# First span's mixers fed through DRAM; the gate projections of both of its blocks as seven-product quads

## The chip, the cores and the metric

The kernel runs on one core of one Trainium2 chip. The metric is the device time of one execution in microseconds (us), lower is better. A core has TensorE (PE; its weight loads are shown apart as PEld), VectorE (DVE), ScalarE (ACT), GpSimd (POOL) and SyncE (SP), which here issues every DMA. SBUF holds the working tiles, PSUM eight banks of 128 x 512 float32, DRAM the inputs, the output and what is put away.

## The reference, cut to what matters

One layer of a streaming encoder, 2048 tokens, width 1024, float32:

```python
xn = rms_norm(x)
aq, ak, av, mq, mk, mv, mo, i, f, ga, gm = split(xn @ w_in)  # 512 x 7, 4, 4, 1024, 1024
A = chunk_band_attention(aq, ak, av, rel_bias)     # 8 heads of 64, own chunk of 64 + 8 before
M = mlstm(silu(conv(mq)), silu(conv(mk)), mv, i, f)          # 4 heads of 128, recurrent
M = sigmoid(mo) * headwise_rms_norm(M)
y = sigmoid(ga) * (A @ w_att_proj) + sigmoid(gm) * (M @ w_mlstm_proj)
x = x + y @ w_out
x = x + relu(rms_norm(x) @ w_up) ** 2 @ w_down
out = rms_norm(x)
```

A and M are 512 wide; ga, gm and y 1024.

## The kernel before

**Blocks and spans.** The 2048 tokens are four blocks of 512 (b = 0 to 3), held feature-major: 128 features on the partitions, 512 tokens along the row. Blocks 0 and 1 are the first span (s = 0), blocks 2 and 3 the second.

**Exactness.** Each float32 operand is split in a high part (rounded to the float32r format) and the rest. A product is three matmuls: high x high, high x low, low x high (`mm3`). A weight tile of 128 x 1024 is loaded into `wraw` (four buffers) and split into `wsp` (three buffers) by one ScalarE and one VectorE pass (lines 427 and 429), in the order that `weights()` lists.

**Two ways to multiply.** A *plain* tile (`feature_tile`, `token_tiles`, `pair_tile`) multiplies one block by one weight tile: 24 matmuls of 128x512 (lines 488 to 490). A *quad* (`quad`, line 571) treats two blocks, two halves of the contraction and two halves of the outputs as a 2 x 2 block product and forms it with seven products for eight. Each of the seven is a weight tile (a sum or difference of four loaded ones, `quad_w`) by an operand (a sum or difference of the four input quarters, A[m][k]); the outputs are sums that `combine` gathers from the banks. One quad gives two output tiles in each half for both blocks, in 7 x 24 = 168 matmuls where plain tiles take 8 x 24 = 192. Its 28 operand tiles lie in `rpool`, which has 28 slots in all.

**Stages.** `dense()` drives TensorE:

1. for b = 0, 1: plain tiles for v, mv, then q, k, mq, mk, mo interleaved (`evac_q`, `evac_k`, `evac_conv`, `evac_og`), then eight plain tiles for ga (`evac_ga`), then the eight projection tiles of A and M (`pair_tile`, with `evac_att` and `evac_rec`), whose results are stored in the DRAM tensor `proj`. Attention (`attention`, `head`, `unit`) and recurrence (`recurrence`, `rec_head`) of the block run beside these tiles, from q, k, v and conv outputs that stay in SBUF slots; block 1 also needs k and v of block 0, which are put away in DRAM (`kspill`, `vspill`);
2. two quads for gm over both blocks (`take_xn`, `after_gate`). Their combining loads the two stored projections, merges them with gm and gives y;
3. two quads for w_out (`take_y`, `after_out`), which add x and store x2;
4. eleven quads or token quads for the whole of w_in on blocks 2 and 3 (`IN_ORDER`, `after_in`, `after_vm`); every result is stored in DRAM (`qfar`, `kfar`, `mvfar`, `mfar`, `gate`);
5. the first span's w_up quads and its w_down products (`down`). Beside `down` run attention and recurrence of blocks 2 and 3, fed from DRAM: `attention_far`, `head_far`, `recurrence_far`, `load_rec`; their results go to DRAM too (`mix`);
6. `project(2)` and `project(3)`: the mixers' results are loaded and split (`take_mix`), projected, merged with the stored gates (`load_gates`, `merge`); under `project(3)` the w_out operands of the second span are formed (`take_y_low`, `take_y_rest`);
7. the second span's w_out, w_up, w_down and final norm (`final`).

**Order.** Every piece of work is a generator that yields what it needs: an engine with an estimated time, a wait for events, or slots of a pool. The class `Flow` runs them at build time as a list scheduler with a clock for each engine and writes the instructions in the order that it finds, so the order on each engine is fixed in the program. Priorities: `dense` has 5 and is passed by work with lower numbers; other threads' matmuls are delayed by a slack of 800 ns after they become ready, so that dense matmuls stand between. Pools: `rpool` 28 slots of two 128x512 parts, `ctx` 16 and `temp` 6 of 128x516 float32, `sc` 4, eight PSUM banks.

Of the kernel before, what the change touches and what calls it, by code (L numbers as in the profile page):

```python
# [44 lines left out]
N_W = 44  # L45
# [4 lines left out]
Q_VM, Q_IN = N_Q, dict(q=N_Q + 2, mq=N_Q + 3, ga0=N_Q + 4, k=N_Q + 5, mk=N_Q + 6, ga1=N_Q + 7, mo=N_Q + 8)  # L50
IN_ORDER = ("gm0", "gm1", "q", "mq", "vm0", "ga0", "k", "vm1", "mk", "ga1", "mo")
# [163 lines left out]
def dve_ns(n):  # L215
    return 70 + 1.042 * n
# [7 lines left out]
class Layer:  # L224
# [99 lines left out]
    def weights(self):  # L324


        part = lambda q, m: ("part", (q, m))
        for b in range(2):
            yield from (("plain", n) for n in range(N_W))
        for q in range(N_G):  # L330
            yield "quad", (q, False)
        yield from (part(q, m) for q in range(N_G, N_G + N_O) for m in range(7))
        for name in IN_ORDER:
            if name[:2] == "vm":
                yield from (part(Q_VM + kk, m) for m in range(7) for kk in range(2))
            else:
                yield "quad", (int(name[2]) if name[:2] == "gm" else Q_IN[name], False)
        for s in range(NS):
# [10 lines left out]
            if s == 0:  # L349
                for _ in range(2):  # L350
                    yield from (("plain", N_W - 8 + 4 * x + j) for j in (0, 2, 1, 3) for x in range(2))
# [277 lines left out]
    def dense(self):  # L629
        fl = self.fl  # L630
        none = [None] * KT
        for b in range(2):
# [3 lines left out]
            fl.spawn(self.attention(b), 1)  # L636
            fl.spawn(self.recurrence(b), 1)
# [12 lines left out]
            yield from self.token_tiles(vs, none, lambda t, bk: self.evac_mv(b, t, bk))  # L650
            self.banks.want = 2
            if b == 0:
                fl.put(self.rpool, *vs)
# [4 lines left out]
            if b == 0:  # L658
                fl.spawn(self.norm_in(1), 3)
# [7 lines left out]
            if b == 1:  # L667
                G = self.operands()
                for k in range(4):
                    fl.spawn(self.take_xn(k, *G), 2)  # L670
            for q in range(N_G, N_G + N_O if b == 0 else 0):
                fl.spawn(self.sum_w(q), 3)
            self.banks.want = 3
            for x, evac in ((0, self.evac_att), (1, self.evac_rec)):
                for j in range(4):
                    yield "wait", B["mix_ev"][4 * x:4 * x + 4]
                    bks = yield from self.pair_tile(B["mix"][4 * x:4 * x + 4], none)
                    for n in range(2):
                        fl.spawn(evac(b, 2 * j + n, bks[n]), 1)
                fl.put(self.rpool, *B["mix"][4 * x:4 * x + 4])  # L680

        self.banks.want = 0
        O, X, U = self.operands(), self.operands(), self.operands()
        for i in range(N_G):
            if i == N_G - 1:
                for k in range(2):
                    fl.spawn(self.take_y(0, k, *O), 2)
            yield from self.quad(*G, self.after_gate(i, O), release=i == N_G - 1)
        for i in range(N_O):
# [5 lines left out]
            yield from self.quad(*O, self.after_out(0, i, None), release=i == N_O - 1)  # L695

        for i, name in enumerate(IN_ORDER):
# [10 lines left out]
            else:  # L708
                yield from self.quad(*X, self.after_in(name), release=last)
        for s in range(NS):  # L710
# [25 lines left out]
            for p, m in enumerate(ORDER):  # L736
                if p == 1:
                    fl.spawn(self.residual(s), 2)
                if s == 0 and p == len(ORDER) - 1:
                    O = self.operands()  # L740
# [4 lines left out]
            if s == 0:  # L745
                yield from self.project(2)
                for k in range(4):
                    fl.spawn(self.take_y_low(k, *O), 2)
                U = self.operands()
                go = Event()  # L750
                first_out = self.after_out(1, 0, U, go)
# [1776 lines left out]
```

## Time and profile before

| what | value |
|---|---|
| time, median of 3 | 2848.65 us |
| lowest and highest | 2846.07 and 2852.96 us |
| the profiled execution's own time | 2843.84 us |
| its span (first to last instruction) | 2842.1 us |
| mean granted TensorE clock | 0.998 |
| busy: PE, PEld | 2804.1, 2342.9 us |
| busy: DVE, ACT, POOL | 2028.9, 1549.7, 48.6 us |
| DMA traffic | 612.03 MB, 215 GB/s |

The profile comes from one execution. Busy time is the time in which an engine has at least one instruction in work; matmuls overlap, so the mean duration of one is longer than their distance. A row of a group names the source line, the engine, the operation, output<-inputs by tile name, the shape and the count, then busy us, mean ns of one, idle us of the engine just before them, and what ended that idle time. In the view of stages every stretch (start:end in us) has the busy time of each engine. Line numbers are those of the kernel before.

### The profile page before, as it was taken

What the parts mean: (1) busy time and instruction counts of PE and PEld (TensorE: products, weight loads), DVE (VectorE), ACT (ScalarE), POOL (GpSimd) and SP (SyncE); (2) the same over time, 40 slices, a digit from 0 to 9 for tenths busy, and PEclk for the clock granted to TensorE, in tenths of its full rate; (3) what the DMA queues carried; (4) which work ended last, traced back from release to release, by engine and by line L of the source; (5) the groups of instructions that cost most, each with busy time, mean ns of one, the idle gap of its engine ahead of it and who ended that gap; (6) DMA issues with size and microseconds to landing.
All of it is one profiled execution on the core that took longest, in us unless ns stands there. A gap on an engine that the chain in (4) does not pass through costs nothing.

```text
span 2842.1 us, 39060 instructions
## 1 busy us (share of the span) xinstructions
PE 2804.1 (99%) x13576; PEld 2342.9 (82%) x13576; DVE 2028.9 (71%) x3767; ACT 1549.7 (55%) x2677; POOL 48.6 (2%) x108
## 2 busy tenths in 40 slices
PE   8999999999999999999999999999999999999998
PEld 7888888888878887888887888888887888888887
DVE  6886478877896766886667788889578644455565
ACT  4664366755444535575556566665435655555444
POOL 0000000000000000000000000000000000000000
PEclk9999999999999999999999999999999999999999
DMA  6337733367756677588778977866597655566563
GB/s 213 100 96 247 254 99 103 104 212 238 263 196 210 205 258 242 195 296 310 265 270 270 283 237 225 249 217 219 204 306 230 213 200 194 198 238 212 188 223 134
DMA packets 280869, 612.03 MB, mean 215 GB/s; under 512 B 31456, under 2 KB 47968, under 8 KB 280672
## 3 DMA queue, kind: packets, MB, share of 16 engines
q1 hardware_dynamic: 280672, 609.55, 65.0%
q8 instruction: 106, 1.74, 0.3%
q14 instruction: 91, 0.75, 0.1%
HBM read 431.17 MB, written 178.26 MB: 214 GB/s over the span
## 4 chain that ended last, share of the span: by engine, by line
PE 80%; DVE 9%; DMA 5%; ACT 3%; issue 2%; POOL 0%; SPq 0%; POOLq 0%; DVEq 0%; ACTq 0%
PE bank L571 36%; PE bank L488 12%; PE bank L489 12%; PE bank L490 12%; PE bank L1243 2%; DVE wsp L429 2%; PE bank L1314 2%; PE bank L1283 1%; DMA wsum<-ctx 1%; DVE sc L1289 1%; ACT wsp L427 1%; DMA ctx<-in_wf 1%; DMA r<-u 1%; PE bank L599 1%; DVE r L1319 1%
## 5 line engine op out<-in xcount | busy, mean ns | idle before, releaser
L571 PE MATMUL bank<-r,wsp 128*128 128x512 f32 x5208 | 1188.6, 390 | 4.6 <-DVE ctx L1837 2.2
L571 PEld LDWEIGHTS bank<-r,wsp 128*128 128x128 f32 x5208 | 975.7, 188 | 210.6 <-DVE ctx L1837 3.8
L429 DVE TENSOR_TENSOR wsp<-wraw,wsp 128x1024 fp32r<-128x1024 f32 x461 | 563.2, 1222 | 352.5 <-ACT wsp L427 336.0
L427 ACT CAST wsp<-wraw 128x1024 fp32r<-128x1024 f32 x461 | 483.8, 1050 | 468.6 <-PE bank L571 196.7
L488 PE MATMUL bank<-r,wsp 128*128 128x512 f32 x1600 | 639.8, 400 | 2.3 <-ACT tmp L2379 2.3
L490 PE MATMUL bank<-r,wsp 128*128 128x512 f32 x1600 | 625.0, 391 | 0.0
L489 PE MATMUL bank<-r,wsp 128*128 128x512 f32 x1600 | 624.6, 390 | 0.0
L490 PEld LDWEIGHTS bank<-r,wsp 128*128 128x128 f32 x1600 | 300.3, 188 | 64.8
L488 PEld LDWEIGHTS bank<-r,wsp 128*128 128x128 f32 x1600 | 301.0, 188 | 54.4 <-ACT tmp L2379 3.0
L489 PEld LDWEIGHTS bank<-r,wsp 128*128 128x128 f32 x1600 | 301.4, 188 | 51.4
L986 ACT CAST r<-r 128x512 fp32r<-128x512 f32 x240 | 146.4, 621 | 86.2 <-DMA r<-u 71.5
L991 DVE TENSOR_TENSOR r<-r 128x512 fp32r<-128x512 f32 x240 | 160.3, 687 | 38.4 <-ACT r L986 37.3
L1837 DVE TENSOR_TENSOR ctx<-bank,ctx 128x512 f32<-128x512 f32 x174 | 119.0, 687 | 81.1 <-PE bank L571 79.3
L1298 ACT ACTIVATE sc<-sc,scs 128x640 f32<-128x640 f32 (+4 forms) x128 | 97.5, 762 | 85.1 <-DVE scs L1295 82.6
L1829 ACT COPY ctx<-bank 128x512 f32<-128x512 f32 x174 | 101.1, 582 | 61.5 <-PE bank L571 54.8
L2198 ACT ACTIVATE ctx<-ctx 128x512 f32<-128x512 f32 x96 | 60.6, 631 | 103.0 <-DVE ctx L1837 103.0
L396 DVE TENSOR_TENSOR ctx<-ctx,ctx 128x512 f32<-128x512 f32 x112 | 76.3, 688 | 55.4 <-DMA ctx<-in_wf 39.8
L1289 DVE CUSTOM_DVE_ANT_0 sc<-bank,bias 128x320 f32<-128x320 f32 (+3 forms) x240 | 105.4, 460 | 12.2 <-PE bank L1283 9.7
L1243 PE MATMUL bank<-r,r 128*128 128x256 f32 (+1 forms) x672 | 109.2, 283 | 4.6 <-DVE r L1319 3.5
L1243 PEld LDWEIGHTS bank<-r,r 128*128 128x128 f32 x672 | 99.2, 191 | 16.6 <-DVE r L1319 7.0
L1319 DVE TENSOR_TENSOR r<-bank,r 128x512 fp32r<-128x512 f32 (+1 forms) x168 | 96.3, 594 | 17.0 <-ACT r L1317 16.1
L1317 ACT CAST r<-bank 128x512 fp32r<-128x512 f32 (+1 forms) x168 | 81.7, 518 | 25.1 <-PE bank L1314 23.1
(291 smaller groups left out, 2850.2 us busy)
## 6 DMA issues: line engine op xcount, KB each, us to landing
wraw<-in_wf SPq DMA_DIRECT2D x170, 512.0 KB, 4.2
wraw<-wsum SPq DMA_DIRECT2D x136, 512.0 KB, 4.0
r<-u SPq DMA_DIRECT2D x224, 256.0 KB, 4.1
wraw<-in_w SPq DMA_DIRECT2D x104, 512.0 KB, 3.9
u<-ctx SPq DMA_DIRECT2D x128, 256.0 KB, 2.6
ctx<-in_wf SPq DMA_DIRECT2D x112, 256.0 KB, 3.9
wsum<-ctx SPq DMA_DIRECT2D x112, 256.0 KB, 4.3
u<-tmp SPq DMA_DIRECT2D x96, 256.0 KB, 3.0
```

The costliest lines, as they stand in the source:

```text
L427: nc.scalar.copy(w[:, 0], raw)
L429: nc.vector.tensor_sub(w[:, 1], raw, w[:, 0].bitcast(F32))
L488: mm(ps, lh, rh, start=first, stop=False)
L489: mm(ps, lh, rl, start=False, stop=False)
L490: mm(ps, ll, rh, start=False, stop=last)
L571: mm(ps, wv[:, x, k, n], a[:, y], start=new and k == 0 and x == y == 0, stop=k == 3 and x == 1, skip_group_check=True)
L986: self.nc.scalar.copy(dst[:, 0], src)
L991: self.nc.vector.tensor_sub(dst[:, 1], src, dst[:, 0].bitcast(F32))
L1243: nc.tensor.matmul(bk[:, c0:c0 + w], st, sl[:, x, o:o + w], start=n == 0, stop=n == total - 1)
L1289: nc.vector.tensor_tensor_reduce(out=e[:, x * w:x * w + w], in0=bks[x][:, :w], in1=br[:, j0 + x * w:j0 + x * w + w], op0=ALU.add, op1=ALU. ...
L1319: nc.vector.tensor_sub(slot[:, 1, :o], bk[:, :o], slot[:, 0, :o].bitcast(F32))
L1837: nc.vector.tensor_add(t[:, o:o + 512], ps, t[:, o:o + 512])
```

## The change

- **Blocks 0 and 1 use the far mixers.** `attention`, `head`, `evac_q`, `evac_k`, `spill_k`, `recurrence` go; `attention_far`, `head_far`, `recurrence_far`, `load_rec` serve all four blocks. After their plain tiles, v, q, k, mv, the conv outputs and mo are stored in DRAM (`evac_v`, `evac_parts`, `evac_mv`, `evac_conv` with `conv_far`, `evac_og`) and loaded per head. The tiles' order changes: q and k first, then the conv inputs, then mo; block 1's mv tiles come after its q and k. The conv's history and the recurrence's gates are chained over all blocks in the same way.
- **ga as quads.** The 16 plain ga tiles go. Four quads, ga0, ga1, gm0, gm1, run over both blocks (`GATES`), from the operands that gm alone used; they are loaded in two parts (`take_low` for the first two products, `take_rest`).
- **Block 0's projection** runs after both blocks' dense tiles and is stored raw (`keep_proj`). The combining of gm loads it with the stored ga and merges the three (`merge_kept`).
- **Block 1's projection** runs after the four quads by `project(1)`, as in the second span, and `project_span` holds what both spans now share.
- **norm_in(1)**, the first norm of block 1, is spawned before block 0's q and k tiles, in `ctx` instead of `sc`, and takes its `rpool` slots one by one (`x_room`) instead of waiting for block 0's.

The core of the diff:

```diff
         for b in range(2):
...
-            fl.spawn(self.attention(b), 1)
-            fl.spawn(self.recurrence(b), 1)
+            fl.spawn(self.attention_far(b), 1)
+            fl.spawn(self.recurrence_far(b), 1)
...
             for j in range(4):
-                for fn in (self.evac_q, self.evac_k, self.evac_conv_q, self.evac_conv_k, self.evac_og):
+                for name in ("q", "k"):
                     (bk,) = yield from self.feature_tile(xs, none if b > 0 or j > 0 else B["xs_done"])
-                    fl.spawn(fn(b, j, bk), 1)
...
+                    fl.spawn(self.evac_parts(b, j, name, bk), 1)
+            if b > 0:
+                yield from self.token_tiles(vs, none, lambda t, bk: self.evac_mv(b, t, bk))
+            for j in range(4):
+                for g in (j, MH + j):
+                    (bk,) = yield from self.feature_tile(xs, none)
+                    fl.spawn(self.evac_conv(b, g, bk), 1)
...
-            for j in range(8):
+            for j in range(4):
                 (bk,) = yield from self.feature_tile(xs, none)
-                fl.spawn(self.evac_ga(b, j, bk), 1)
+                fl.spawn(self.evac_og(b, j, bk), 1)
...
+        fl.spawn(self.take_mix(0), 1)
+        for j in (0, 2, 1, 3):
+            for x in range(2):
+                some = slice(4 * x, 4 * x + 4)
+                bks = yield from self.pair_tile(self.blk[0]["mix"][some], self.blk[0]["mix_ev"][some])
+                for n in range(2):
+                    fl.spawn(self.keep_proj(x, 2 * j + n, bks[n]), 1)
...
-        for i in range(N_G):
-            if i == N_G - 1:
-                for k in range(2):
-                    fl.spawn(self.take_y(0, k, *O), 2)
-            yield from self.quad(*G, self.after_gate(i, O), release=i == N_G - 1)
+        for name in GATES:
+            last = name == GATES[-1]
+            if last:
+                fl.spawn(self.take_mix(1), 1)
+            yield from self.quad(*G, self.after_in(name, 0), release=last)
+        O, first_out = yield from self.project_span(0, None)
...
+    def merge_kept(self, j, t):
...
+        yield "wait", [self.proj_ev[0][j], self.proj_ev[1][j], self.g_ev[0, 0, j]]
+        got = yield "get", self.temp, 3
+        m, a, g = (x[:, :512] for x in got)
+        for to, src in ((m, self.projd.ap()[1, j]), (a, self.projd.ap()[0, j]), (g, self.gd[0].ap()[0, j])):
+            yield "sp", 900, 3000
+            nc.sync.dma_start(to, src)
+        yield "dve", dve_ns(512)
+        nc.vector.scalar_tensor_tensor(t5, t5, 1.0, m, op0=ALU.add, op1=ALU.mult)
+        yield "dve", dve_ns(512)
+        nc.vector.scalar_tensor_tensor(a, g, 1.0, a, op0=ALU.add, op1=ALU.mult)
+        yield "dve", dve_ns(512)
+        nc.vector.tensor_add(t5, t5, a)
...
+    def project_span(self, s, U):
...
+        O = self.operands()
+        if s > 0:
+            yield from self.project(2 * s)
+        for k in range(4):
+            fl.spawn(self.take_low(k, *O, self.ypd[2 * s], self.yp_ev[2 * s], 0.5), 2)
+        go = Event()
+        after = self.after_out(s, 0, U, go)
+        for k in range(4):
+            fl.spawn(self.take_rest(k, *O, self.ypd[2 * s:2 * s + 1], self.yp_ev[2 * s:2 * s + 2], 0.5, self.y3[s]), 1)
+        yield from self.project(2 * s + 1, go)
+        return O, after
```

`head_far` now loads the k of every block by its two halves:

```diff
-        for n, x in ((0, b - 1), (1, b)):
-            if x < 2:
-                yield "wait", [self.blk[x]["k_spilt"][h]]
-                yield "sp", 900, 2000
-                nc.sync.dma_start(kf[:, n], self.kdram[x].ap().bitcast(F32)[h])
-            else:
-                yield "wait", [self.k_ev[x, j]]
-                yield "sp", 900, 2000
-                for a in range(2):
-                    nc.sync.dma_start(kf[a * 64:a * 64 + 64, n], self.kfar[x].ap()[j, a, rows])
+        for n, x in ((0, b - 1), (1, b)) if b > 0 else ((1, b),):
+            yield "wait", [self.k_ev[x, j]]
+            yield "sp", 900, 2000
+            for a in range(2):
+                nc.sync.dma_start(kf[a * 64:a * 64 + 64, n], self.kfar[x].ap()[j, a, rows])
```

More of the change, by code (lines that the diff above doesn't have):

```diff
@@ L44 @@
 NS = NB // 2
-N_W = 44
+N_W = 36
 N_G, N_O, N_F = 2, 2, 8
@@ L50 @@
 Q_VM, Q_IN = N_Q, dict(q=N_Q + 2, mq=N_Q + 3, ga0=N_Q + 4, k=N_Q + 5, mk=N_Q + 6, ga1=N_Q + 7, mo=N_Q + 8)
+GATES = ("ga0", "ga1", "gm0", "gm1")
 IN_ORDER = ("gm0", "gm1", "q", "mq", "vm0", "ga0", "k", "vm1", "mk", "ga1", "mo")
@@ L349, in weights @@
             if s == 0:
-                for _ in range(2):
-                    yield from (("plain", N_W - 8 + 4 * x + j) for j in (0, 2, 1, 3) for x in range(2))
+                yield from proj + proj
     def loader(self):
@@ L708, in dense @@
             else:
-                yield from self.quad(*X, self.after_in(name), release=last)
+                yield from self.quad(*X, self.after_in(name, 1), release=last)
         for s in range(NS):
@@ L1578, in rec_head @@
+        yield from self.store(self.mfar[b].ap()[2 * MH + h], d5, self.m_ev[b, 2 * MH + h], self.ctx, dst)
     def rec_head(self, b, h):
@@ L2463, in _layout @@
         tiles += [feat(w_in, _X[n] + j * P) for n in ("q", "k", "mq", "mk", "mo")]
-    tiles += [feat(w_in, _X["ga"] + j * P) for j in range(8)]
     for w in (w_att, w_ml):
```

534 lines of the change are left out of this document (162 added, 372 removed).

## The prediction

> **What bounds the kernel now.** I read the page first: the totals by engine and the chain that ended last.
>
> ```profile
> span 2842.1 us, 39060 instructions
> PE 2804.1 (99%) x13576; PEld 2342.9 (82%) x13576; DVE 2028.9 (71%) x3767; ACT 1549.7 (55%) x2677; POOL 48.6 (2%) x108
> ...
> PEclk9999999999999999999999999999999999999999
> ...
> PE 80%; DVE 9%; DMA 5%; ACT 3%; issue 2%; POOL 0%; SPq 0%; POOLq 0%; DVEq 0%; ACTq 0%
> ```
>
> TensorE works from end to end at the full granted clock, and stands idle for 2842.1 - 2804.1 = 38.0 us in all. The other engines count only where they make it wait. So two things are to be found: how many matmuls go, at what pace, and where the new order makes TensorE wait. For both I cut the span by stage; the borders come from the timeline of TensorE. Columns: stretch, its length, then busy us and instructions of PE, PEld, DVE, ACT, POOL, then granted clock, share of the DMA engines and GB/s.
>
> ```profile
> 80.00:215.00 135.00, 133.53 (x759) 114.36 (x758) 113.62 (x333) 92.33 (x224) 8.18 (x20) 1.00 0.30 95
> ...
> 380.00:556.00 176.00, 174.96 (x1024) 152.62 (x1023) 152.08 (x426) 123.04 (x277) 11.61 (x19) 1.00 0.32 104
> ...
> 645.00:721.00 76.00, 76.00 (x337) 62.94 (x336) 64.27 (x88) 42.45 (x66) 0.00 (x0) 1.00 0.78 254
> 721.00:797.00 76.00, 76.00 (x344) 62.96 (x343) 68.51 (x98) 33.27 (x47) 0.00 (x0) 1.00 0.70 238
> ...
> 1520.00:1950.00 430.00, 422.25 (x2419) 365.03 (x2418) 350.43 (x945) 270.21 (x593) 12.55 (x36) 1.00 0.79 243
> 1950.00:2128.00 178.00, 174.59 (x839) 146.00 (x838) 121.50 (x173) 77.31 (x111) 3.25 (x2) 1.00 0.74 249
> 2128.00:2216.00 88.00, 85.60 (x375) 69.70 (x374) 76.70 (x113) 51.40 (x77) 0.00 (x0) 1.00 0.71 231
> ```
>
> In order: attention of block 0 (its first to its last score), attention of block 1, the two gm quads of the first span, its two w_out quads, attention and recurrence of blocks 2 and 3 (fed through DRAM), their projections with the end of the down products, and the w_out quads of the second span. The second span already runs the form that the change gives to the first, so it is the nearest row for nearly every new cost.
>
> **The matmuls.** A plain tile is 24 matmuls of 128x512 (8 k by 3 products), a quad 7 products x 2 x 4 x 3 = 168. Out go 8 ga tiles in each of two blocks, 16 x 24 = 384; in come two quads (ga0, ga1), 336. That is 48 fewer, and the order of instructions of the two kernels shows the same: 10,008 against 9,960 with a weight tile as stationary operand (13,218 against 13,170 in all). The other forms only change the tile that they read: the same 128x128, 128x129 and score shapes in the same numbers. The pace comes from the purest stretch, the gm quads: 76.00 us for 337 matmuls, 225.5 ns each. So 48 x 0.2255 = **-10.8 us**, all on the path, since TensorE has no other bound there.
>
> The Trainium skill, "TensorE: Matmul & The Clock Gate", section "Back-to-back issue gap", gives some 131 ns for each 512-column matmul in a sustained stream with weight loads; by that figure the 48 would be worth an estimated 6.3 us. The trace disagrees with it, at 225.5 ns for these operands, and the trace decides.
>
> **Mixers through DRAM.** Block 0's and block 1's q, k, v, conv outputs and gates are stored and loaded again (`attention_far`, `recurrence_far`), as blocks 2 and 3 do now. Who waited for whom, TensorE only, in blocks 2 and 3's mixers; of that view, the longest three rows and the DMA's other one:
>
> ```profile
> PE bank L1609 <- DMA r<-mfar: 1.0, 1, 1.0
> PE bank L1243 <- ACT r L1317: 0.9, 1, 0.9
> PE bank L1424 <- DVE cum L1420: 0.9, 1, 0.9
> ...
> PE bank L1627 <- DMA r<-mvfar: 0.2, 1, 0.2
> ```
>
> The loads themselves cost TensorE 1.2 us over 16 heads and 8 recurrence heads: they are issued early enough, and between them stand dense matmuls. The rest are short waits on VectorE and ScalarE. In all, the stretch 1520 to 1950 is idle for 7.75 us, 1.80 per 100 us; the two near stretches for 1.47 + 1.04 = 2.5 us, 0.81 per 100.
>
> How long are the new stretches? In the changed order 264 dense matmuls lie between block 0's first and last score where 396 lay, and 360 where 447 lay for block 1 (the ga tiles and block 0's projection have left). So they shrink by 132 x 0.2255 = 29.8 and 87 x 0.2255 = 19.6 us, to 105.2 and 156.4. At the second span's rate 261.6 us have 4.7 us idle, 2.2 more than now. Bounds: the near rate on the shorter stretches, 2.1, so -0.4; and all 7.75, so +5.2. I take **+2.2**, as the code is that of the second span.
>
> VectorE is what gets tight. Rows of its groups in 80 to 556 us (weight splits, and the split of a mixer's output that now leaves for DRAM), and five of its fullest slices:
>
> ```profile
> L429 DVE TENSOR_TENSOR wsp<-wraw,wsp 128x1024 fp32r<-128x1024 f32 x63 | 77.0, 1222 | 51.9 <-ACT wsp L427 50.6 <-PE bank L1609 0.8
> ...
> L1267 DVE TENSOR_TENSOR r<-tmp,r 64x256 fp32r<-64x256 f32 x29 | 12.1, 417 | 1.6 <-ACT r L1265 1.1
> ```
> ```profile
> 80.00:100.00 20.00, 19.89 (x112) 16.86 (x111) 18.87 (x59) 14.68 (x33) 1.18 (x5) 1.00 0.35 108
> 160.00:180.00 20.00, 19.82 (x107) 16.48 (x106) 19.15 (x66) 14.13 (x34) 1.31 (x3) 1.00 0.32 98
> 200.00:220.00 20.00, 19.11 (x105) 16.18 (x104) 18.99 (x67) 13.27 (x32) 1.30 (x3) 1.00 0.30 93
> 480.00:500.00 20.00, 19.57 (x112) 16.99 (x112) 20.00 (x62) 14.82 (x30) 1.61 (x3) 1.00 0.26 84
> 1920.00:1940.00 20.00, 19.87 (x111) 16.91 (x110) 19.64 (x45) 14.68 (x27) 0.00 (x0) 1.00 0.50 165
> ```
>
> Block 0's stretch loses 132/24 = 5.5 weight splits of 1.222 us and 16 output splits of 0.417, 13.4 us: 113.62 - 13.4 = 100.2 us of VectorE in 105.2, 95% where it is 84% now. Block 1 loses 3.6 splits and 16, 11.1 us: 141.0 in 156.4, 90% (86% now). The slices say what such a share costs: with VectorE at 94 to 100%, TensorE lost 0.11 + 0.18 + 0.89 + 0.43 + 0.13 = 1.74 us in 100, the rate already taken.
>
> **Projections and w_out quads.** Now the first span's projections end block by block, and its gm and w_out quads run without a gap (76.00 of 76.00, twice). After the change block 0's projection is kept raw (`keep_proj`), four quads run, and `project_span` does block 1's projection and forms the w_out operands under it (`take_low`, `take_rest`), as `project(3)` does today. What that costs is seen behind `project(3)`; waits of TensorE in 2128 to 2216 us, then of the stage before it:
>
> ```profile
> PE bank L571 <- ACT r L988: 1.5, 1, 1.5
> PE bank L571 <- DVE ctx L2082: 0.5, 1, 0.5
> PE bank L571 <- DVE r L993: 0.4, 1, 0.4
> ```
> ```profile
> PE bank L488 <- ACT tmp L2379: 2.3, 2, 1.2
> PE bank L1243 <- DVE r L1319: 1.1, 1, 1.1
> ```
>
> The first fence is 2.4 us: operands from `take_y_rest`, split last, reach the third product late. I take **+2.4**; bounds 0 (the gap-free quads now) and 4.7, with the 2.3 behind L2379, which is the final norm's output of the first span and has no counterpart earlier. `merge_kept` has 8 x 3 VectorE passes and 24 loads inside two gm quads; its last low result is needed only after the whole of `project(1)`, 192 x 0.2255 = 43.3 us later, so I cost it at nothing. If its loads were that late, each microsecond over 43 would be one of the span.
>
> **Queues.** SP issues 2,168 transfers instead of 1,912, some 50 MB more. The rows of the kinds that multiply (KB each, median us from issue to landing):
>
> ```profile
> r<-mfar SPq DMA_DIRECT2D x24, 256.0 KB, 4.9
> r<-kfar SPq DMA_DIRECT2D x48, 128.0 KB, 4.3
> ...
> r<-kspill SPq DMA_DIRECT2D x16, 256.0 KB, 5.0
> ...
> r<-mvfar SPq DMA_DIRECT2D x8, 256.0 KB, 6.3
> ```
>
> The mixer stretches move 95 and 104 GB/s at a DMA share of 0.30 to 0.32, the second span 243 at 0.79, so there is room; a store that waits on SP holds the weight loads behind it, but three split weight tiles are 3 x 24 x 0.2255 = 16.2 us of matmuls, more than any landing here. So I cost them at zero.
>
> A head's k now comes in two loads of 128 KB, one for each half of the partitions, instead of one of 256 (kspill). If the second only follows the first, it is 2 x 4.3 - 5.0 = 3.6 us later; no row shows whether it does, and in blocks 2 and 3 it stays hidden behind matmuls.
>
> The Trainium skill, "DMA: Bandwidth & Descriptors", section "Rules for kernel authors", speaks against such pairs: two transfers to disjoint halves of the partitions serialize, and one over all 128 should be used. By it the 3.6 us are there.
>
> One added wait stands early: in the changed order VectorE's passes over the stored ga gates (`merge_kept`) follow the sums of ga0's second product, though they belong to gm0. They wait for a store and a load.
>
> ```profile
> gate<-ctx SPq DMA_DIRECT2D x32, 256.0 KB, 2.6
> r<-qfar SPq DMA_DIRECT2D x32, 256.0 KB, 6.1
> tmp<-gate SPq DMA_DIRECT2D x32, 256.0 KB, 4.5
> ```
> ```profile
> L1837 DVE TENSOR_TENSOR ctx<-bank,ctx 128x512 f32<-128x512 f32 x174 | 119.0, 687 | 81.1 <-PE bank L571 79.3
> ...
> L2006 ACT ACTIVATE ctx<-ctx 128x512 f32<-128x512 f32 x30 | 18.7, 628 | 22.1 <-DVE ctx L1837 22.0
> ```
>
> With the sum (0.69) and the tanh (0.63) that is 8.4 us from the product's end. Queued behind on VectorE are the weight split of the seventh product, four products or 4 x 24 x 0.2255 = 21.6 us ahead of its use, and the sums of the fifth, 16 us ahead. Nothing.
>
> **The sum.** -10.8 + 2.2 + 2.4 = -6.2 us; bounds -10.8 - 0.4 + 0 = -11.2 and -10.8 + 5.2 + 4.7 = -0.9. The profiled execution took 2843.84 us, its span 2842.1 with 1.7 around it, and 4.8 less than the median 2848.65 of the three timed runs (2846.07 to 2852.96). So 2837.6 for a like execution, and **2842.4** for a median.
>
> **Rivals.**
> *The first span copies the second, stalls and all.* Mixers idle the full 7.75 us and both fences of the projections recur, -0.9 us, 2847.8. For it: same code, denser mixers. Against: the 2.3 come from a neighbour that the first span lacks. Chance 0.13.
> *The halves of k serialize and show* at the first head of each block, where nothing is loaded ahead: 2 x 3.6 over my sum, +1.0, 2849.7. Against: the whole DMA wait of blocks 2 and 3 is 1.2 us. Chance 0.07.
> *VectorE decides, and it is slower.* Its idle 16% in block 0 (1 - 113.62/135) and 14% in block 1 may be forced, by hops TensorE to VectorE to ScalarE and back. If neither stretch can go under them, they take 100.2/0.84 = 119.3 and 141.0/0.86 = 164.0, 14.1 and 7.6 us over my lengths: -6.2 + 21.7 = +15.5, 2864.2. It decides from +11.9 us over my sum, an idle share of about 12%: 8.7 + 3.8 = 12.5. Against: the slices with 94 to 100%, but those are 20 us long, not 105. Chance 0.12.
> *Every new stall is hidden and the old ones go too.* -10.8 - 2.5 = -13.3, 2835.4; for it the gap-free quads, against it that VectorE gets fuller. Chance 0.18.
> That the 48 matmuls don't go is excluded by the order of instructions.
>
> **How the numbers follow.** My sum has 0.50. What a measurement of this kernel can tell from no change is about 0.2%, 5.7 us. Of my own 0.50, bounds -11.2 to -0.9, 0.32 lie beyond -5.7 and 0.18 within; the first two rivals are within (0.13 + 0.07), the third is slower (0.12), the fourth faster (0.18): faster 0.50, same 0.38, slower 0.12. The range: from the fourth rival less the spread of the runs, 2835.4 - 2.6 = 2833, to 2849.7 plus their spread upward of 4.3 and a little of the third, 2855; outside are most of the slower case and some of the tails.
>
> **What would show it.** Right: dense pace near 225 ns; TensorE idle of 4 to 5 us over blocks 0 and 1's mixers with VectorE over 90% in block 0; a wait of 1 to 3 us on operands of the first w_out quad; nothing in the four gate quads. Wrong: TensorE waiting on score or transpose results (L1289, L1319 of now) for over 10 us before 450 us; waits on kfar, qfar or mvfar loads over 1 us each; idle at the third product of the ga0 quad, whose operands wait for slots.

## The result, and the profile after

The changed kernel takes 2863.94 us (median of 6 runs, 2861.34 to 2871.45) against 2848.76 for the kernel before (2845.16 to 2854.19, 6 runs): 1.0055 times as long, 95% interval 1.0038 to 1.0072. The forecast was 2842.4. The profiled execution took 2863.24 us.

From the page of the changed kernel, the totals and the chain that ended last:

```profile
span 2861.4 us, 39400 instructions
PE 2802.6 (98%) x13528; PEld 2337.2 (82%) x13528; DVE 2016.3 (70%) x3745; ACT 1529.6 (53%) x2639; POOL 48.1 (2%) x100
...
PE 72%; DVE 13%; DMA 9%; ACT 3%; issue 2%; SPq 1%; POOL 0%; POOLq 0%; DVEq 0%; ACTq 0%
```

48 matmuls fewer, a mean granted clock of 0.997 for 0.998, yet TensorE's idle time rose from 38.0 to 2861.4 - 2802.6 = 58.8 us, and its share of the chain fell from 80% to 72% while VectorE and DMA gained. The stretches that answer to those of the prediction (columns as there; from here on line numbers are those of the kernel that a view belongs to, the changed one unless another is named):

```profile
97.70:204.20 106.50, 102.02 (x606) 87.73 (x606) 98.12 (x307) 72.45 (x176) 7.57 (x18) 1.00 0.79 244
309.10:459.30 150.20, 146.61 (x868) 128.45 (x867) 130.15 (x378) 98.17 (x212) 7.55 (x16) 1.00 0.71 218
204.20:309.10 104.90, 100.38 (x490) 81.39 (x490) 59.72 (x153) 40.84 (x95) 5.03 (x7) 0.97 0.85 276
459.30:533.70 74.40, 71.13 (x370) 60.03 (x369) 55.13 (x115) 48.59 (x114) 5.95 (x5) 0.98 0.70 232
533.70:687.20 153.50, 152.61 (x673) 126.05 (x672) 91.76 (x109) 73.60 (x114) 1.01 (x1) 1.00 0.61 203
687.20:730.80 43.60, 43.60 (x194) 36.09 (x194) 36.23 (x51) 16.07 (x23) 0.00 (x0) 1.00 0.80 266
```

In order: attention of block 0 and of block 1, the rest of the plain tiles behind each (where the recurrences end), the four gate quads, block 1's projection. The first four end 533.7 us into the span; in the kernel before the gate quads began at 644.5. Up to there TensorE has 1,536 weight-tile matmuls for 2,112, so at 225.5 ns this part should have shrunk by 129.9 us and shrank by 110.8: **19.1 us are lost there.** TensorE's idle time in the four stretches is 4.5 + 3.6 + 4.5 + 3.3 = 15.9 us, as much outside the attention stretches as in them; in the kernel before, the two attention stretches had 2.5. The clock column has 0.97 and 0.98 in the two stretches behind: 4.5 of the 19.1 us are lost by a halved clock right behind the two longest waits (last section).

I cut every trace at two borders, the first gate quad and the first token quad of the second span (vm0), take off the weight-tile matmuls of each stage at 225.5 ns, and compare what is left with the kernel before:

| | first gate quad | first vm0 quad | last matmul | stage 1, lost | stage 2 | stage 3 |
|---|---|---|---|---|---|---|
| before | 644.5 | 963.0 | 2833.1 | | | |
| changed | 533.7 | 976.3 | 2852.5 | +19.1 | +5.1 | +6.0 |

With the 10.8 us of the matmuls that is 30.2 - 10.8 = 19.4 us, the whole difference of the traces. Stage 1 is the mixers with the plain tiles beside them, stage 2 the gate quads, projections, the first span's w_out quads and the second span's first w_in quads, stage 3 all that follows.

**What TensorE waits for in stage 1.** The longest rows of before (75 to 645 us), then of the changed kernel (90 to 700):

```profile
PE bank L1243 <- DVE r L1319: 2.1, 6, 0.9
PE bank L1314 <- DVE tmp L1255: 0.4, 1, 0.4
PE bank L1627 <- DVE ctx L1611: 0.4, 1, 0.4
```
```profile
PE bank L1521 <- DVE cst L1524: 4.7, 4, 2.2
PE bank L1519 <- DVE ctx L1507: 3.6, 2, 3.4
PE bank L1196 <- DVE r L1263: 2.3, 6, 0.6
PE bank L1258 <- DVE tmp L1208: 1.9, 2, 1.2
```

Not one is a load: every wait is for VectorE, the longest in the recurrence (`rec_head`, lines 1507 to 1524). But VectorE is busy for 57 and 74% of those tails, so why is it late? Its own timeline around the 3.4 us (start, length, instruction, idle before and what ended it), and TensorE's across the stall:

```profile
217.16 0.16 DVE L1433 CAST r<-ones 128x4 fp32r<-128x4 f32 x1
222.52 0.69 DVE L404 TENSOR_TENSOR ctx<-ctx,ctx 128x512 f32<-128x512 f32 x1 [5.19 <-DMA ctx<-in_wf]
...
225.28 0.17 DVE L1433 CAST r<-ones 128x4 fp32r<-128x4 f32 x1
228.66 0.69 DVE L404 TENSOR_TENSOR ctx<-ctx,ctx 128x512 f32<-128x512 f32 x1 [3.22 <-DMA wsum<-ctx]
229.27 1.22 DVE L437 TENSOR_TENSOR wsp<-wraw,wsp 128x1024 fp32r<-128x1024 f32 x1
230.41 1.28 DVE L404 TENSOR_TENSOR ctx<-ctx,ctx 128x512 f32<-128x512 f32 x2
231.61 0.68 DVE L1507 SCALAR_TENSOR_TENSOR ctx<-bank,ctx 128x512 f32<-128x512 f32 x1
```
```profile
228.12 0.39 PE L496 MATMUL bank<-wsp,r 128*128 128x512 f32 x1
228.34 0.39 PE L497 MATMUL bank<-wsp,r 128*128 128x512 f32 x1
228.57 0.39 PE L498 MATMUL bank<-wsp,r 128*128 128x512 f32 x1
232.35 0.80 PE L1519 MATMUL bank<-r,ctx 128*128 128x129 f32 x2 [3.39 <-DVE ctx L1507]
```

VectorE stands still for 8.4 us, first for a load and then for a store of L404, which is `sum_w`: sums of w_out's quarters that nobody needs for another 500 us. The order on VectorE is fixed, so L1507 stands behind them, and TensorE behind L1507. Work without urgency that waits for a landing holds work that is urgent. The next longest, the 2.2 us on L1524 (at 481 us), begins with a landing too, with one engine more between: VectorE stood behind ScalarE's splits, and ScalarE had stood 1.46 us for a load of block 0's stored mixer outputs (`take_mix`). VectorE waited for `sum_w`'s loads in the kernel before too (80 to 580 us), but beside block 0's projection and ga tiles, and TensorE's waits above show hardly anything of it:

```profile
DVE ctx L396 <- DMA ctx<-in_wf: 12.5, 4, 5.5
```

### The profile page after: what moved, and what is told of

It is laid out like the page before. It is cut to its first block, busy times and chain, and to the rows that moved or that the text cites. A ratio compares the mean times of both kernels' runs of the same rounds, so it can differ in the third digit from the quotient of the medians.

```text
span 2861.4 us, 39400 instructions
## 1 busy us (share of the span) xinstructions
PE 2802.6 (98%) x13528; PEld 2337.2 (82%) x13528; DVE 2016.3 (70%) x3745; ACT 1529.6 (53%) x2639; POOL 48.1 (2%) x100
## 4 chain that ended last, share of the span: by engine, by line
PE 72%; DVE 13%; DMA 9%; ACT 3%; issue 2%; SPq 1%; POOL 0%; POOLq 0%; DVEq 0%; ACTq 0%
PE bank L579 32%; PE bank L496 10%; PE bank L497 10%; PE bank L498 10%; DVE wsp L437 3%; PE bank L607 2%; PE bank L1196 2%; DMA wsum<-ctx 2%; DVE r L1037 2%; DMA r<-u 1%; PE bank L1258 1%; PE bank L1227 1%; ACT wsp L435 1%; DVE sc L1233 1%; DMA ctx<-in_wf 1%
## 5 line engine op out<-in xcount | busy, mean ns | idle before, releaser
L579 PE MATMUL bank<-r,wsp 128*128 128x512 f32 x5544 | 1266.4, 390 | 11.7 <-DVE ctx L1686 6.7
L496 PE MATMUL bank<-r,wsp 128*128 128x512 f32 x1472 | 588.8, 400 | 3.0 <-DVE tmp L1208 1.8
L498 PE MATMUL bank<-r,wsp 128*128 128x512 f32 x1472 | 575.4, 391 | 0.0
L497 PE MATMUL bank<-r,wsp 128*128 128x512 f32 x1472 | 575.1, 391 | 0.0
L1032 ACT CAST r<-r 128x512 fp32r<-128x512 f32 x264 | 161.0, 622 | 85.7 <-DMA r<-u 66.8
L1037 DVE TENSOR_TENSOR r<-r 128x512 fp32r<-128x512 f32 x264 | 175.8, 686 | 35.0 <-ACT r L1032 33.5
L1686 DVE TENSOR_TENSOR ctx<-bank,ctx 128x512 f32<-128x512 f32 x186 | 126.8, 686 | 84.8 <-PE bank L579 83.8
L1678 ACT COPY ctx<-bank 128x512 f32<-128x512 f32 x186 | 108.0, 582 | 71.0 <-PE bank L579 65.2
L404 DVE TENSOR_TENSOR ctx<-ctx,ctx 128x512 f32<-128x512 f32 x112 | 76.6, 690 | 61.4 <-DMA ctx<-in_wf 40.8
L454 DVE TENSOR_TENSOR wraw<-wraw,wraw 128x1024 f32<-128x1024 f32 x76 | 92.6, 1219 | 5.3 <-DMA wraw<-in_wf 3.7
```

The source lines that it names most:

```text
L496: mm(ps, lh, rh, start=first, stop=False)
L497: mm(ps, lh, rl, start=False, stop=False)
L498: mm(ps, ll, rh, start=False, stop=last)
L579: mm(ps, wv[:, x, k, n], a[:, y], start=new and k == 0 and x == y == 0, stop=k == 3 and x == 1, skip_group_check=True)
L1032: self.nc.scalar.copy(dst[:, 0], src)
L1037: self.nc.vector.tensor_sub(dst[:, 1], src, dst[:, 0].bitcast(F32))
```

## The experiments

Theory A: VectorE's and SP's fixed orders hold the mixers' chains up behind instructions that wait for landings, and with less dense work beside the mixers TensorE feels it. Its rivals: the way through DRAM costs this whatever stands beside it; VectorE has too much to do; the planner's order is merely another throw.

All results, with the losses by stage of the profiled execution against the kernel before (as in the table above; one execution each, so a few us of it are not more than that):

| kernel | median us | ratio to before, interval | stage 1 | 2 | 3 |
|---|---|---|---|---|---|
| changed | 2863.94 | 1.0055, 1.0038 to 1.0072 | +19.1 | +5.1 | +6.0 |
| e1, sums later | 2867.99 | 1.0065, 1.0042 to 1.0089 | +11.4 | +13.9 | +8.7 |
| e3, lead 1600 | 2856.49 | 1.0024, 1.0010 to 1.0037 | +11.7 | +4.7 | +8.3 |
| e4, short conv | 2865.29 | 1.0050, 1.0030 to 1.0069 | +18.3 | +4.3 | +9.5 |
| e5, w_out as quads | 2856.46 | 1.0033, 1.0021 to 1.0044 | +13.9 | +3.6 | +7.3 |
| e6, later landings | 2877.17 | 1.0107, 1.0092 to 1.0122 | +13.0 | +9.5 | +19.7 |
| e2b, ga plain | 2861.34 | 1.0051, 1.0037 to 1.0066 | +5.5 | +8.1 | +3.4 |
| e9, e5 and lead | 2838.81 | 0.9977, 0.9968 to 0.9987 | +2.2 | +5.0 | -0.8 |
| e10, e5 and rest later | 2855.02 | 1.0033, 1.0019 to 1.0048 | +11.3 | +5.0 | +9.2 |
| e11, all three | 2844.07 | 0.9989, 0.9977 to 1.0002 | +3.4 | +6.8 | -2.6 |
| e12, e10 and norm later | 2856.27 | 1.0038, 1.0023 to 1.0053 | +12.0 | +6.8 | +4.5 |
| e14, e9, lead in first span | 2846.55 | 0.9998, 0.9988 to 1.0009 | +0.1 | +4.6 | +7.6 |
| e8, before with lead 1600 | 2846.28 | 0.9993, 0.9984 to 1.0003 | -0.3 | +0.2 | +2.9 |
| e13, before with e9's edits | 2845.11 | 0.9994, 0.9985 to 1.0004 | -5.1 | +5.0 | +5.7 |

**The sums, later (e1).** Spawned ahead of the gate quads instead of behind block 0's tiles:

```diff
-            for q in range(N_G, N_G + N_O if b == 0 else 0):
-                fl.spawn(self.sum_w(q), 3)
...
         self.banks.want = 0
+        for q in range(N_G, N_G + N_O):
+            fl.spawn(self.sum_w(q), 3)
```

> The sums of w_out's quarters (sum_w for its two quads) start before the four gate quads instead of beside block 0's last recurrence heads; nothing else changes. Theory A (VectorE and SP, each in a fixed order, hold each other up beside the mixers): the 8.4 us for which VectorE stands behind the loads and stores of these sums at 217 to 229 us go, and with them the 3.4 us wait of TensorE on L1507 and its neighbours: 4 to 7 us faster than the changed kernel, 2857 to 2860. Theory B (the loads of the far mixers themselves come too late): no change, 2862 to 2866.

Stage 1 gained 7.7 us, stage 2 lost 8.8 and stage 3 2.7. TensorE's two longest rows, 90 to 700 us: the gate quads now wait for their combining (L1686), and block 1's tail is hit as well. Below them what VectorE stood for ahead of the 4.0 us:

```profile
PE bank L579 <- DVE ctx L1686: 7.6, 4, 4.0
PE bank L1258 <- DVE ctx L1556: 3.5, 1, 3.5
```
```profile
563.45 1.22 DVE L454 TENSOR_TENSOR wraw<-wraw,wraw 128x1024 f32<-128x1024 f32 x1 [4.04 <-DMA wraw<-in_wf]
```

That is not one of the moved sums but a sum in a weight buffer (`quad_w`) that waited for its load; ahead of the 3.5 us VectorE stood 2.65 us for a load of `take_rest`. So other instructions that wait for landings held TensorE in the sums' place. How far the moved sums' transfers made these loads late is not shown. The 2857 to 2860 was missed; one hold had been taken for the whole cause.

**More lead (e3; e8 on the kernel before).** The planner lets a mixer's matmul become due `SLACK` after its operands are ready, and so puts more dense matmuls ahead of it:

```diff
-    SLACK = 800.0
+    SLACK = 1600.0
```

> The slack by which a mixer's matmul is put later than the planner has it ready goes from 800 to 1600 ns, for the whole kernel. Theory A in the form that VectorE is late by jitter of about a microsecond, with room behind: the waits of 0.5 to 1.5 us go, 5 to 10 us faster than the changed kernel, 2854 to 2859. In the form that VectorE is full for 100 us on end: lateness adds up whatever the slack, 2861 to 2866. Theory B expects what the first form does, for loads that are late by a microsecond.

The ratio falls from 1.0055 to 1.0024, within the forecast of the first form, and stage 1 loses 7.4 us less: late VectorE results cost less where more stands ahead. The same edit on the kernel before:

> The kernel before, with the planner's lead of TensorE's mixer instructions raised from 800 to 1600 ns, as in the run of the changed kernel that gained 7.5 us by it. Theory A (the lead helps where the mixers lack dense work beside them): before has more of it, so it gains 0 to 2 us, 2846 to 2850 us. Rival E (the lead helps any kernel with this planner, so what was gained is no sign of the change's cost): it gains 5 to 8 us, 2840 to 2844 us.

Nothing there (0.9993, the interval holds 1). So the lead heals something that the change brought.

**Less work for VectorE (e4).** Blocks 0 and 1 form one of the conv's three shifted products; two are left out.

```diff
-        for n in range(3):
+        for n in range(3 if b > 1 else 1):
```

> Leaves out two of the three shifted products of the conv in blocks 0 and 1: 16 x 2 VectorE passes of 0.67 us, 21 us of VectorE beside the mixers; all else stays. Theory A in the form that VectorE's work is the bound beside the mixers: 5 to 10 us faster than the changed kernel, 2854 to 2859. In the form that VectorE stands still behind DMA in its queue, and theory B: 0 to 3 us faster, 2861 to 2864.

No gain to speak of, with VectorE's busy time 14.8 us lower (2001.5 us); the longest hold even grew:

```profile
PE bank L1519 <- DVE ctx L1507: 6.5, 1, 6.5
```

So the amount of VectorE work alone is not the bound; its order changed here too.

**No separate sums (e5).** The first use of w_out forms its sums in the weight buffers as the up quads do (`quad_w`), and keeps them for the second span:

```diff
-        yield from (part(q, m) for q in range(N_G, N_G + N_O) for m in range(7))
+        for q in range(N_G, N_G + N_O):
+            yield "quad", (q, True)
...
-            for q in range(N_G, N_G + N_O if b == 0 else 0):
-                fl.spawn(self.sum_w(q), 3)
```

> The changed kernel, but the sums of w_out's quarters are formed in the weight buffers when the first span's w_out quads are loaded (as the up quads' are), and kept from there for the second span; the separate sums beside block 0's mixers, whose loads VectorE waited for (3.2 and 5.2 us), are gone. Theory S (these sums alone hold VectorE, and with it TensorE, at 200 to 300 us): the stalls of 9.5 us there fall to about 2, nothing comes in their place, 2855 to 2858 us. Theory A (VectorE and SP stand in one fixed order each, and any instruction that waits for a load holds what stands behind it; without as much dense work beside the mixers TensorE feels it): a part of the gain comes back as stalls elsewhere, as in the run with the sums put later, 2859 to 2865 us.

2856.46, within theory S's figures (the ratio fell from 1.0055 to 1.0033), but with theory A's mark: stage 1 still loses 13.9 us. The stall at 228 us is gone; the longest TensorE row (90 to 700 us) is now in block 1's tail, and VectorE's row for the same time (430 to 520 us) names the next instruction of the same kind, `take_rest`'s loads:

```profile
PE bank L1257 <- DVE ctx L1555: 3.6, 1, 3.6
```
```profile
DVE ctx L1615 <- DMA ctx<-xn: 5.9, 2, 3.2
```

**Telling the planner of later landings (e6).** All `yield "sp", 900, 2000` and `900, 3000` become `900, 4500` (and one wait more for the loads of x beside the first w_out quad).

> The changed kernel, with the planner told that a load or store of 128x512 lands 4.5 us after its issue instead of 2 or 3 us (the trace has 4 to 6 us); one wait is added for the loads of x beside the first w_out quad, so that they do not take the buffers of y. The order of the instructions follows from the planner, so each engine's order changes with it. Theory A (the orders rest on landings that are too early, so engines wait in order for loads): the excess over the pace between 100 and 560 us falls from 31 to 15 to 20 us, 2847 to 2856 us. Rival D (the stalls come from how the work is packed beside the mixers, not from landings): within 3 us of the changed kernel, 2861 to 2867 us.

The worst of all. Stage 1 loses 6.1 us less, stage 2 4.4 and stage 3 13.7 more, of which 6.3 are half clock (last section); presumably what depends on a landing is now put later everywhere. That orders matter is borne out; that truer landing times in the planner would mend them is not.

**Half the change (e2b).** ga stays 16 plain tiles, the rest is the change, with the one wait that e6 adds too. (A form with these tiles behind the mo tiles, e2, has no result: its planner came to a point where no piece of work could go on.)

```diff
-GATES = ("ga0", "ga1", "gm0", "gm1")
+GATES = ("gm0", "gm1")
...
-            yield from rows(2, 3) + rows(4)
+            yield from rows(2, 3) + [("plain", 28 + j) for j in range(8)] + rows(4)
...
+            for j in range(8):
+                (bk,) = yield from self.feature_tile(xs, none)
+                fl.spawn(self.evac_ga(b, j, bk), 1)
```

> One part of the change alone: the first span's mixers go through DRAM and block 0's projection is kept raw and merged late, but both blocks' ga stays 16 plain tiles of 24 matmuls in the dense part, as before (48 matmuls more than the changed kernel, 10.9 us; the two ga quads beside nothing are gone). One wait is added for the loads of x beside the first w_out quad. Theory A (the mixers' tails stall TensorE because less dense work stands beside them, and the plain ga tiles put 87 us of it back): the excess between 100 us and the end of the dense part falls from 31 to 12 to 18 us, 2857 to 2866 us. Rival B (the way through DRAM costs this whatever stands beside it): the excess stays at 30, 2871 to 2877 us.

Stage 1 loses 5.5 us instead of 19.1: the same way through DRAM, the same sums, but 2 x 8 plain tiles more beside them. For stage 1 that speaks for theory A and against the rival that the way itself costs it. There the plain tiles that left, replaced by quads that save 48 matmuls (10.8 us), cost 13.6 us. But the total, 2861.34, can't be told from the changed kernel's, and with as many matmuls as the kernel before e2b takes 1.0051 of its time: stages 2 and 3 lose 8.1 and 3.4 us. For those no cause is shown, so the rival is open there.

**The two edits together (e9)** (no separate sums, lead 1600), and the same on the kernel before (e13):

> The changed kernel with two of the earlier edits together: w_out's sums formed in the weight buffers, and the planner's lead raised to 1600 ns. Theory A (each takes away part of the same loss, which sits beside the first span's mixers): 2850 to 2853 us, about 4 us over before. Rival F (a planner with another order throws new dice each time, so gains don't add): 2854 to 2862 us.

> The kernel before with the two edits that together brought the changed kernel to 2838.8 us: w_out's sums formed in the weight buffers, and the lead of 1600 ns. Theory A (the edits undo what the change did to the first span; before, with block 0's projection and 8 ga tiles beside its mixers, hardly has that loss): within 3 us of before, 2844 to 2849 us, so that the change with both edits is worth 6 to 10 us against it, near the 10.9 us of its matmuls. Rival E (the edits help this planner anywhere): 2833 to 2841 us, and the change is worth nothing or loses even when both are prepared alike.

2838.81 us, faster than both kernels, by more than forecast. The chain, TensorE's longest waits (90 to 700 us) and the attention stretches:

```profile
PE 82%; DMA 7%; DVE 6%; ACT 2%; issue 2%; SPq 0%; POOL 0%; POOLq 0%; DVEq 0%; ACTq 0%
```
```profile
PE bank L1257 <- DVE sc L1245: 2.2, 3, 0.8
PE bank L1195 <- DVE r L1262: 1.5, 2, 0.7
PE bank L497 <- DVE scs L1232: 1.1, 1, 1.1
```
```profile
92.40:207.50 115.10, 113.53 (x665) 98.65 (x664) 104.80 (x319) 77.31 (x181) 8.38 (x19) 1.00 0.78 246
291.50:463.90 172.40, 166.93 (x979) 145.16 (x978) 143.57 (x398) 114.35 (x254) 11.20 (x18) 1.00 0.70 222
```

The waits on L1507 and L1524 (1506 and 1523 here) are gone, and stage 1 loses 2.2 us. VectorE still waits for landings (6.7 us for `take_rest`'s loads, 90 to 700 us), but no wait of TensorE is longer than 1.1. The attention stretches are 8.6 and 22.2 us longer than in the changed kernel while the span is 24 us shorter, and have 7.0 us idle for 8.1: a longer stretch costs nothing by itself, as dense matmuls fill it. On the kernel before the two edits together give 0.9994, no difference in the whole, though its stage 1 gains 5.1 us, which stages 2 and 3 give back (+5.0, +5.7). So in the whole they take away a loss that the change brought. With them on both, the change is worth some 5 us by the ratios (0.9977 and 0.9994, whose intervals just touch), under the 6 to 10 forecast; and in stage 1, prepared alike, it still costs 2.2 + 5.1 = 7.3.

**Where the lead acts (e14).** As e9, but `fl.SLACK = 800.0` from the gate quads on:

> As the run with w_out's sums in the weight buffers and the lead of 1600 ns, but the lead goes back to 800 ns once the gate quads begin, so that only the first span's mixers have it. Theory A (the lead matters where the mixers' chains run beside too little dense work, in the first span): the excess from 0 to 700 us stays near the 19.6 us of that run (31.6 with the lead at 800), 2840 to 2846 us. Rival F (the gain is how the second half's order happened to fall): 2850 to 2857 us.

The time is just above theory A's 2840 to 2846. Stage 1 stays at +0.1, and 2846.55 is 10 us under e5: the lead in the first span does that. In stage 1 the kernels with a lead of 800 there lose 19.1 us with the separate sums and 13.9, 11.3 and 12.0 without (e5, e10, e12); with 1600 it is 11.7 with them and 2.2, 3.4 and 0.1 without (e9, e11, e14). That is too regular for a mere throw of the planner, though each is one execution. The other 8 us of e9 lie in stage 3 (-0.8 against +7.6), where the instructions are the same and only the lead, and so the order, differs. Over the kernels with a lead of 1600 there (e3, e9, e11, e8, e13) stage 3 goes +8.3, -0.8, -2.6, +2.9, +5.7: no rule. Of e9's 8.4 us there, 3 lie in two more windows of half clock in e14 (last section); what makes the orders differ was not tried and stays open, and so it stays open how much of e9's lead over the kernel before is more than a lucky order there.

**Two edits that did not help:** `take_rest` behind block 0's projection on top of e5 (e10), and block 1's norm begun after block 0's q and k tiles on top of that (e12); e11 is e10 with the lead:

```diff
-        for k in range(4):
-            fl.spawn(self.take_rest(k, *G, self.xnd[:2], self.xn_kept[:2], 1.0), 2)
...
         fl.put(self.rpool, *self.blk[0]["mix"])
         self.banks.want = 0
+        for k in range(4):
+            fl.spawn(self.take_rest(k, *G, self.xnd[:2], self.xn_kept[:2], 1.0), 2)
...
-            if b == 0:
-                fl.spawn(self.norm_in(1), 2)
...
+            if b == 0:
+                fl.spawn(self.norm_in(1), 3)
```

> The changed kernel with w_out's sums formed in the weight buffers, and the loads and sums of the gate quads' operands (take_rest) put behind block 0's projection instead of ahead of it. In the run with the sums moved, VectorE waited twice for these loads (5.9 us in all) while block 1's recurrence was still going, and TensorE stalled 11.4 us at 450 to 500 us. Theory A: those stalls fall to about 4, and the gate quads start late by 0 to 3 us: 2849 to 2854 us. Rival: the operands are late for the gate quads and TensorE waits for them: 2856 to 2862 us, with the wait at the first gate quads.

> As the run with w_out's sums in the weight buffers and take_rest later, and block 1's input norm is begun after block 0's q and k tiles, with the last priority, as in the kernel before it stood late (its loads held VectorE beside block 0's attention, where TensorE lost 7.6 us at 100 to 200 us). Theory A: the stalls there fall to 3 to 4 us, 2845 to 2851 us. Rival: block 1's operands come late and TensorE waits for them at the end of block 0's tiles: 2852 to 2860 us.

> The three edits together: w_out's sums in the weight buffers, take_rest behind block 0's projection, lead 1600 ns. Theory A: 2844 to 2850 us, about even with before (the 10.9 us of matmuls saved are then just given back in the second half's stalls and what is left of the first). Rival F (gains don't add): 2852 to 2860 us.

2855.02 and 2856.27, no better than e5; stage 1 goes to +11.3 and +12.0 from +13.9, but stages 2 and 3 of e10 lose 3.3 more. TensorE's row of 3.6 us on L1555 stays, at 3.5 in e10, and VectorE's timeline there says why: `take_rest`, though spawned later, still stands ahead of L1555 and waits for its loads. The edit did not move it out of block 1's tail, so e10 says nothing against these loads as the cause.

```profile
PE bank L1257 <- DVE ctx L1555: 3.5, 1, 3.5
```
```profile
451.83 1.42 DVE L1615 TENSOR_TENSOR ctx<-ctx,ctx 128x512 f32<-128x512 f32 x2 [2.88 <-DMA ctx<-xn]
...
453.57 0.68 DVE L1555 TENSOR_TENSOR ctx<-bank,r 128x512 f32<-128x512 f32 x1
```

e11 took 2844.07 us, within theory A's 2844 to 2850, but behind e9: an edit that gained nothing alone added nothing to it.

## Why the prediction was wrong

- **The matmuls, -10.8: right.** 48 fewer went, at the pace used: block 1's projection has 194 in 43.60 us, 224.7 ns. (The Trainium skill, "TensorE: Matmul & The Clock Gate", "Back-to-back issue gap", has 131 ns; these traces disagree with it throughout.)
- **Mixers through DRAM, +2.2, bounds -0.4 to +5.2: wrong, +19.1.** This is the step that failed. The stretches' lengths were right (106.5 and 150.2 us measured, 105.2 and 156.4 forecast), the loads cost TensorE nothing as forecast, and VectorE's 92 and 87% in them were near the 95 and 90. But the sum looked only into the attention stretches; half of the idle time lies behind them, in 179 us that I had costed at nothing, where the dense tiles had been thinned as well. And the second span's rate was no guide: beside its mixers (1520 to 1950 us of the kernel before) VectorE has two passes of `sum_w` (1.4 us, without a wait) and no `take_rest`. Instructions that wait for landings, in a fixed order, were not in the sum at all. Nor was what a long wait costs behind itself: the sum took the full clock throughout, and 4.5 of the 19.1 us are half clock. That stage 1 comes to +2.2 with the two edits, the number of the prediction, is luck: the same edits take 5.1 us off the kernel before, so prepared alike stage 1 costs 7.3, beyond the upper bound of 5.2 (one execution each).
- **Projections and w_out quads, +2.4, bounds 0 to 4.7: mis-sized**, stage 2 took +5.1. The forecast wait came, at the first w_out quad (1.5 us, below), and the gate quads lost 153.5 - 672 x 0.2255 = 2.0, where nothing was forecast; the other 1.6 lie elsewhere in the stage.

```profile
PE bank L579 <- ACT r L1034: 1.5, 1, 1.5
```

- **Queues, zero: right for TensorE, which hardly waits for a load, but the wrong question.** Landings that VectorE awaits are what holds it, and the sum never asked for them. They did not grow: the DMA share in block 0's stretch went from 0.30 to 0.79, yet VectorE's waits for `sum_w`'s transfers are 8.5 + 5.1 us here and were 12.5 + 1.4 before (90 to 700 and 75 to 645 us). What changed is what they hold up.
- **merge_kept's early wait, nothing: nearly right.** VectorE waited for its loads (90 to 700 us), and TensorE in the gate quads and block 1's projection (533 to 735 us) only once, on a quad's sums:

```profile
DVE tmp L785 <- DMA tmp<-proj: 5.3, 4, 2.8
...
DVE tmp L785 <- DMA tmp<-gate: 4.0, 2, 2.4
```
```profile
PE bank L579 <- DVE ctx L1686: 0.9, 1, 0.9
```

- **The halves of k** (rival): the only wait of TensorE for a load that the view of the whole span lists is another one:

```profile
PE bank L1505 <- DMA r<-mfar: 1.2, 1, 1.2
```

  Whether the halves serialize, as the Trainium skill, "DMA: Bandwidth & Descriptors", "Rules for kernel authors", states, no run here shows.
- **Behind, +6.0, not forecast.** The second half's instructions are the same; 5.1 us of it are idle time of TensorE, and why they arose is open.
- **The VectorE rival** gave 2864.2, the time that came, for a reason that did not: its longer stretches (119.3 and 164.0 us) did not appear, taking VectorE work away gained nothing, and in e9 stretches about as long (115.1 and 172.4 us) go with the shortest time.

## What to carry to other kernels

In a program whose order on each engine is fixed, look for instructions that wait for a transfer and are not urgent, and for what stands behind them on their engine; removing them beat moving them here (1.0033 and 1.0065). Dense work that is taken away beside latency-bound chains is worth its own time less the stalls that it hid: ask of each such tile what it covers, up to the end of the chains and not of the busiest stretch. In a trace, read the granted clock behind long waits too, not only the idle time. When a planner's orders are in play, judge an edit with the same planner settings tried on both kernels.

## What the runs showed of the hardware

TensorE's idle time understates what a wait costs. Stage 1 of before and of the changed kernel:

```profile
0.00:644.50 644.50, 633.91 (x3304) 534.35 (x3305) 474.03 (x1178) 374.06 (x776) 29.84 (x64) 1.00 0.48 158
```
```profile
0.00:533.70 533.70, 510.35 (x2728) 429.98 (x2729) 402.81 (x1088) 306.85 (x672) 27.90 (x55) 0.99 0.76 243
```

It rose from 10.6 to 23.4 us, 12.8, where the stage lost 19.1. Most of the rest is the clock. The wait of 3.4 us ends at 232.35 us, and from 231.1 to 237.9 the granted clock is 0.50; behind the 2.2 us (to 483.15) it is 0.50 again, from 483.7 to 487.1. Matmuls of the same shape in the first window and behind it:

```profile
231.10:237.90 6.80, 5.55 (x17) 4.72 (x18) 2.61 (x6) 1.82 (x4) 0.00 (x0) 0.50 1.01 319
```
```profile
235.50 0.63 PE L497 MATMUL bank<-wsp,r 128*128 128x512 f32 x1
235.93 0.63 PE L498 MATMUL bank<-wsp,r 128*128 128x512 f32 x1
...
240.50 0.39 PE L497 MATMUL bank<-wsp,r 128*128 128x512 f32 x1
240.73 0.39 PE L498 MATMUL bank<-wsp,r 128*128 128x512 f32 x1
```

They start 0.43 us apart in it and 0.23 behind it, and count as busy in both. The two windows, 10.2 us at half clock, cost 5.1 us, 0.6 of them while TensorE still stood: 4.5 of the 19.1. Over all fifteen traces, behind the first load and ahead of the program's end, 36 of 45 such windows begin during a wait of TensorE of 1.5 us or more or within 3.5 us of its end, and 16 of the 19 waits of 2.5 us or more have one; no edit tried the clock by itself. The runs agree: the mean granted clock is 0.995 to 0.997 in all six of the changed kernel, 0.997 to 0.999 in e9's ten, 0.992 to 0.994 in e6's four.

The last 1.8 us may be record length: a matmul's record is 0.39 us long at a distance of 0.23, so some 0.16 us of each wait lie under the record of the matmul ahead (an estimate; a dozen waits would make up the 1.8).

A higher DMA share did not lengthen every landing. The weight tiles and the loads of `sum_w`, before (80 to 380 us, 50.6% of the queue's time) and changed (97 to 310 us, 81.6%), KB each and median us from issue to landing:

```profile
wraw<-in_w SPq DMA_DIRECT2D x44, 512.0 KB, 3.8
...
ctx<-in_wf SPq DMA_DIRECT2D x16, 256.0 KB, 4.7
```
```profile
wraw<-in_w SPq DMA_DIRECT2D x26, 512.0 KB, 4.7
...
ctx<-in_wf SPq DMA_DIRECT2D x15, 256.0 KB, 4.8
```
